# Hybrid RG-LRU and differential-attention block: k and q of heads 0 and 1 projected while the input arrives

## Chip, cores and metric

One core of a Trainium2 chip. The time is device microseconds of one launch; of several runs the median is given.

## What is computed

One decoder block on x, 2048 tokens of 1024 channels, float32. The reference, cut to its core:

```python
u = rmsnorm(h, pre_g[l])
z = einsum('bsd,df->bsf', u, w_in[l])                    # 1024 -> 8 x 1024
xr, zr, q, k, v, za, gm = split(z)                       # gm has 2 x 1024
y_r = rg_lru(causal_conv4(xr), ...) * silu(zr)           # gates from 64 x 64 blocks, scan over tokens
o   = diff_attention(q, k, v, lam)                       # 8 heads, causal: softmax(q0 k0) - lam softmax(q1 k1)
y_a = rmsnorm(o, subln_g[l]) * (1 - lam_init) * silu(za)
g_r, g_a = split(sigmoid(gm))
m = g_r * (y_r @ w_br_rnn) + g_a * (y_a @ w_br_attn)
h = h + rmsnorm(m @ w_out, post_g[l])
```

## The kernel before

Every large product is done in three fp16 products (high x high, high x low, low x high), so that 128 output channels by 512 tokens cost 3 x 8 = 24 matmuls of 512 columns (`mm3`, L187). Such a set is called a group here; done on 128 tokens at a time it is four pieces of 24 matmuls of 128 columns. Engines have short names: PE (matmul), DVE (vector), ACT (scalar), POOL (GpSimd), SP (its queue issues most transfers).

The work runs in four stages.

1. x phase. x comes in 16 tiles of 128 tokens, loaded five ahead. `x_stat` squares two tiles on ACT (L256) and turns the sums to scales on DVE, `x_fin` scales them on DVE (L266), makes the high half on ACT and the low half on DVE or POOL in turns (L270), and SP transposes both into `uT` (L276). Meanwhile PE works the first half row (8 tiles) of three blocks, x_r 0, z_r 0 and x_r 1, in pieces of 128 tokens (`in_half`, list `first`). Small constants, the LRU's gate weights (`gf`, `gw`) and the parameters (`rows`, `prm`) are loaded between the tiles.
2. LRU. Sixteen units, one for each block of 128 channels and half row: `xr_half` (48 matmuls of 512), convolution, `gates` (12 float32 matmuls), `zr_half` (48 matmuls), then the scan and the product. PSUM holds three tiles of 1024 (`lps`), each free once ACT and DVE have read it. Each unit also brings on one weight block: load (`wld`), norm on ACT (`wstat`, L156), scale by a one-column matmul (L162) and split into halves on ACT and DVE (`wfin`, L177, L178). The last loads are the first of the attention (`ahead`).
3. Attention. 128 units, one for each head and 128 queries: scores, exponentials, combination, transposes of the weights by DMA (`pt`), and the product with v two units later (`LAG`). Between them stand the remaining groups of the input projection, in a list `fills`: per head and chunk of 512 tokens k, q and two of v and za (`chunk_groups`), and the merge gates gm, 64 groups in all, of which 8 wait for the end. A running sum `acc` deals them out evenly over the units. A k or q group is split to fp16 halves (`split16`, L667, L668) and moved into K and Q by four or six transfers on SP. gm is written to DRAM.
4. Branch projections, merge and output projection from L1094 on.

The code is written in this order, but a scheduler orders the instructions of each engine; each engine then runs its own list strictly in that order and waits where an operand is missing.

Of the kernel before, what the change touches and what calls it, by code (L numbers as in the profile page):

```python
# [48 lines left out]
def kernel(  # L49
# [35 lines left out]
    gm_d = drp.tile([2 * KD, 128, S], F32, name="gm_d")  # L85

# [7 lines left out]
    with ExitStack():  # L94
# [65 lines left out]
        def w_scale(w, ps, fac, keep=None):  # L160
            """power of two that brings the block's norm close to 2^13 (a rough sum is enough for it)"""
            nc.tensor.matmul(ps[:, 0:1], ones16, w.ss, start=True, stop=True)  # L162
            tot = tl(1, "w_tot")
            nc.vector.tensor_scalar(out=tot, in0=ps[:, 0:1], scalar1=1e-30, scalar2=None, op0=ALU.max)
            w.sg, w.iv = keep or (tl(1, f"w_sg_{w.tag}"), tl(1, f"w_iv_{w.tag}"))
            pow2_bits(w.sg, tot, 13)
            pow2_inv(w.iv, w.sg)
            if keep is None:
                w.cz = wn_p.tile([128, 1], F32, tag=f"w_cz_{w.tag}", name="w_cz",
                                 bufs={"wg": 4, "agm": 3}.get(w.tag, 2))  # L170
                nc.vector.scalar_tensor_tensor(out=w.cz, in0=w.iv, scalar=fac, in1=cu, op0=ALU.mult, op1=ALU.mult)
# [15 lines left out]
        def mm3(ps, w, c0, n):  # L187
            """ps[f128, n] += w^T u over all of d, s in [c0, c0 + n)"""
# [7 lines left out]
        # ================= RG-LRU branch =================  # L196
        with ExitStack() as lx:
# [21 lines left out]
            def prep_g(gr):  # L219
                """power of two that keeps the scaled, normalised input in fp16's range"""  # L220
# [58 lines left out]
            # weight pipeline  # L279
            order = [(C_XR if i % 2 == 0 else C_ZR) + (i // 2) * 128 for i in range(2 * KD)]  # L280
            ahead = [("k", 0), ("q", 0), ("v", 0), ("za", 0)]
            order += [wkey_col(k) for k in ahead]
            ws = {}

            def wld(i):
                ws[i] = w_load(win, order[i], tag="wg" if i < 2 * KD else "a" + ahead[i - 2 * KD][0])
# [4 lines left out]
            def wfin(i):  # L291
                w_fin(ws[i], lpt.tile([128, 1], F32, tag="tot", name="tot"), 0.5 if i % 2 and i < 2 * KD else 1.0,
                      w16_at(i))

            first = []

            def in_half(b, hf, z, w):
                """PSUM tile of a half row of an x_r (z = 0) or z_r (z = 1) block"""
                if hf == 0 and 2 * b + z < 3:
                    if not first:  # L300
                        first.extend(lps.tile([128, HALF], F32, tag="ps", name="ps") for _ in range(3))
                        for i in range(HALF // 128):
                            for y_ in range(3):
                                mm3(first[y_][:, i * 128:(i + 1) * 128], ws[y_], i * 128, 128)
                    return first[2 * b + z]
# [3 lines left out]
                return ps  # L309

# [125 lines left out]
            with tc.issue_after(x_t[0]):  # L436
                wld(2)
            x_fin(2, 2, gb)
            x_stat(4, 2)
            wstat(2)  # L440
            wfin(2)
            x_fin(4, 2, gb)
            # per-channel vectors: rows of 128 channels, turned into columns
# [10 lines left out]
            x_stat(6, 2)  # L454
            x_fin(6, 2, gb)
            wld(3)
            x_stat(8, 2)
            x_fin(8, 2, gb)
            wstat(3)
            wfin(3)  # L460
# [8 lines left out]
            with tc.issue_after(x_last[1]):  # L469
                # block-diagonal gate weights, exact f32r hi/lo  # L470
# [8 lines left out]
            x_stat(10, 2)  # L479
            x_fin(10, 2, gb)  # L480
            x_stat(12, 2)
            x_fin(12, 2, gb)
            x_stat(14, 2)
            x_fin(14, 2, gb)
# [62 lines left out]
            seq = [(0, 0), (1, 0), (0, 1), (1, 1)] + [(b, hf) for b in range(2, KD) for hf in range(2)]  # L547
            when = {0: 2, 1: 2, 2: 3}
            for n, (b, hf) in enumerate(seq):
                xr_half(b, hf, ws[2 * b])  # L550
# [8 lines left out]
                if n > 0:  # L559
                    if n > 1:  # L560
                        wfin(n + 2)
                    wstat(n + 3)
                wld(n + 4)
                zr_half(b, hf, ws[2 * b + 1])
# [3 lines left out]
                if hf == 1:  # L568
                    ws.pop(2 * b)
                    ws.pop(2 * b + 1)  # L570
# [5 lines left out]
        # ================= differential attention and merge gates =================  # L576
# [3 lines left out]
        with ExitStack() as ax:  # L580
# [16 lines left out]
            wl = {k: ws[2 * KD + i] for i, k in enumerate(ahead)}  # L597
# [16 lines left out]
            def wadv(n):  # L614
                """weight blocks up to index n ready; two more on their way"""
# [16 lines left out]
            sc_h, nsc_h, kap_h = {}, {}, {}  # L632
# [20 lines left out]
            for k in ahead[:2]:  # L653
                after_w(k, wl[k])

# [42 lines left out]

            def g_va(h, c, g):
# [31 lines left out]
            def chunk_groups(h, c):  # L731
                return [("k", h, c), ("q", h, c), ("va", h, c, 0), ("va", h, c, 1)]
# [6 lines left out]
            def W_(nm, h):  # L739
                return [("w", nm, h)] if h < (2 * NH if nm == "gm" else NH) else []  # L740
# [30 lines left out]
            def fill():  # L771
# [5 lines left out]
                if g[0] == "w":  # L777
                    wadv(worder.index((g[1], g[2])))
# [195 lines left out]
        # ================= branch projections, merge, output projection =================  # L974
        with ExitStack() as bx_:
# [179 lines left out]
            # norm of the attention branch's rows, for a bound on the merged sum  # L1155
# [53 lines left out]
```

## Time and profile before

| what | value |
|---|---|
| median of 3 runs | 2503.14 us (2498.83 to 2506.12) |
| time of the first run | 2506.12 us |
| span of the profiled execution | 2506.1 us |
| PE busy | 2353.1 us, 94% |
| DVE, ACT, POOL busy | 62%, 49%, 27% |
| PE's granted clock, mean | 0.980 |
| DMA | 268.73 MB, mean 107 GB/s |

In the rows shown below, a window row gives a stretch in us, its length, then busy time and instructions of PE, PE's weight loads, DVE, ACT and POOL, the clock that PE was granted, the busy share of the DMA engines and GB/s. A timeline row gives start, length, engine, line, operation, out<-in, shapes, count, and in brackets the idle time before it with what ended it. A group row ends in count, then busy us, mean ns of one, idle time before. A transfer row ends in count, size of each and us from issue to landing.

### The profile page before, as it was taken

Reading aid. Unit: us, or ns where it says so; the run is one execution under the profiler, and the core shown is the slowest. Engines: PE = TensorE matmul, PEld = TensorE weight load, DVE = VectorE, ACT = ScalarE, POOL = GpSimd, SP = SyncE. Lnnn points to the kernel's source line nnn. Section 1 sums busy time; section 2 is a strip of 40 time slices with the busy share of each in tenths; the row PEclk is TensorE's granted clock in tenths of the full one; section 3 lists DMA queues with packets and bytes.
Section 4 is the critical chain, followed back from the end, with each engine's and each line's share of the span. In section 5 each row is a group of like instructions: output and inputs, shape, how many; then the busy total and the mean of one; then the engine's idle time right before and its main releaser. Section 6 shows DMA issues by size and latency. Waiting matters only on the chain. (4 is left out here: it accounts for less than half of the span.)

```text
span 2506.1 us, 41430 instructions
## 1 busy us (share of the span) xinstructions
PE 2353.1 (94%) x15240; PEld 1355.3 (54%) x15240; DVE 1548.4 (62%) x4316; ACT 1224.6 (49%) x2156; POOL 679.7 (27%) x415
## 2 busy tenths in 40 slices
PE   6789999999998999998998999999999899999998
PEld 5344444465665665665665655655655444444443
DVE  8877667668658566667567478468467244633323
ACT  5555545456547546556456457356456244312211
POOL 3443334212222212222222222223123133322211
PEclk9899999999999999999999999999999999999999
DMA  9511111235444534635535445445445854743202
GB/s 244 104 43 48 46 42 34 76 81 119 108 96 111 113 84 108 127 82 113 115 84 114 103 96 118 95 90 124 95 90 115 251 177 135 239 148 118 84 17 101
DMA packets 541323, 268.73 MB, mean 107 GB/s; under 512 B 370504, under 2 KB 518016, under 8 KB 541120
## 3 DMA queue, kind: packets, MB, share of 16 engines
q1 hardware_dynamic: 538144, 256.74, 42.6%
q0 software_dynamic: 2816, 9.08, 1.2%
q8 instruction: 119, 1.95, 0.3%
q14 instruction: 84, 0.69, 0.1%
q10 hardware_dynamic: 160, 0.27, 0.0%
HBM read 110.79 MB, written 41.94 MB: 61 GB/s over the span
## 5 line engine op out<-in xcount | busy, mean ns | idle before, releaser
L192 PEld LDWEIGHTS <-w 128*128 128x128 f16 x5040 | 475.9, 100 | 576.5 <-issue 89.2
L192 PE MATMUL mm<-uT,w 128*128 128x512 f16 x3072 | 705.1, 383 | 12.9 <-ACT gm L728 8.9
L877 POOL TENSOR_TENSOR e<-e,e 128x1024 f16<-128x1024 f32 (+2 forms) x192 | 317.0, 1666 | 970.6 <-ACT e L876 487.0
L851 ACT ACTIVATE e<-e,nb,sc_h 128x1024 f32<-128x1024 f32 (+7 forms) x384 | 376.1, 980 | 160.8 <-DVE nb L845 125.6
L826 DVE TENSOR_SCALAR_CACHE_REDUCE e<-sc 128x1024 f32<-128x1024 f32 (+7 forms) x352 | 305.2, 880 | 134.9 <-PE sc L814 122.3
L192 PE MATMUL ps<-uT,w 128*128 128x512 f16 (+1 forms) x1968 | 354.4, 345 | 26.1 <-ACT xr L318 17.7
L711 PE MATMUL mm<-wva,uT 128*128 128x256 f16 x3072 | 352.7, 275 | 3.3 <-DVE st L668 2.6
L1094 PE MATMUL psb<-yt,w 128*128 128x512 f16 x1536 | 332.9, 379 | 2.0 <-ACT w L177 1.5
L711 PEld LDWEIGHTS <-uT 128*128 128x128 f16 x3072 | 301.5, 99 | 48.8 <-issue 2.9
L814 PE MATMUL sc<-K,Q 128*128 128x512 f16 (+3 forms) x1280 | 287.2, 351 | 19.9 <-DVE e L826 13.8
L897 PE MATMUL o<-V,pt 128*128 128x128 f16 x3264 | 224.5, 222 | 38.4 <-DMA pt<-e 38.1
L1094 PEld LDWEIGHTS <-w 128*128 128x128 f16 x1536 | 149.1, 98 | 184.9 <-issue 3.9
L897 PEld LDWEIGHTS <-pt 128*128 128x128 f16 x3264 | 200.0, 99 | 72.8 <-DMA pt<-e 46.5
L876 ACT ACTIVATE e<-e 128x1024 f16<-128x1024 f32 (+2 forms) x192 | 150.1, 802 | 143.1 <-DVE e L874 118.5
L814 PEld LDWEIGHTS <-Q 128*128 128x128 f16 x1280 | 119.6, 99 | 133.2 <-issue 20.2
L874 DVE SCALAR_TENSOR_TENSOR e<-e,rs,e 128x1024 f32<-128x1024 f32 (+2 forms) x192 | 190.0, 1017 | 2.2
L1125 PE MATMUL psf<-wo,m 128*128 128x512 f16 x720 | 155.7, 379 | 0.0
L156 ACT ACTIVATE jk<-wst 128x1024 bf16<-128x1024 f32 x80 | 84.2, 1052 | 138.7 <-DMA wst<-in_w_in_dram 102.6
L1125 PEld LDWEIGHTS <-m 128*128 128x128 f16 x768 | 75.1, 98 | 90.6
L1098 DVE SCALAR_TENSOR_TENSOR t<-gt,psb 128x512 f32<-128x512 f32 x64 | 43.8, 686 | 120.2 <-PE psb L1094 100.1
L1148 ACT ACTIVATE jk<-psf 128x1024 bf16<-128x1024 f32 x15 | 15.4, 1024 | 134.0 <-PE psf L1125 69.4
L717 DVE SCALAR_TENSOR_TENSOR V<-mm,V 128x256 f16<-128x256 f32 x64 | 26.9, 421 | 85.7 <-ACT V L716 85.6
(247 smaller groups left out, 2417.3 us busy)
## 6 DMA issues: line engine op xcount, KB each, us to landing
wst<-in_w_in_dram SPq DMA_DIRECT2D x64, 512.0 KB, 4.5
xt<-in_x_dram SPq DMA_DIRECT2D x32, 512.0 KB, 4.5
gm_d<-gm SPq DMA_DIRECT2D x64, 256.0 KB, 2.7
gt<-gm_d SPq DMA_DIRECT2D x32, 512.0 KB, 3.8
K<-st SPq DMA_DIRECT2D x128, 64.0 KB, 2.0
Q<-st SPq DMA_DIRECT2D x64, 128.0 KB, 2.4
Q<-st SPq DMA_DIRECT2D x128, 64.0 KB, 2.1
ya_d<-yT SPq DMA_DIRECT2D x64, 128.0 KB, 2.0
```

The lines of the kernel that those rows point to most:

```text
L156: nc.scalar.activation(jk, w.st, AF.Square, accum_out=ss)
L192: nc.tensor.matmul(ps, w.t[:, a, k, :], uT[:, b, k, c0:c0 + n], start=(i == 0), stop=(i == 3 * KD - 1))
L711: nc.tensor.matmul(ps[:, j, :], uT[:, a, k, s0:s0 + 128], wt[:, b, k].rearrange("p t f -> p (t f)"), start=(i == 0), stop=(i == 3 * KD - 1))
L814: nc.tensor.matmul(ps[:, x * 128:x * 128 + m], Qt[h, t // 4][:, v, ci, q0:q0 + 128], K[:, ci, 0:m], start=(v == 0), stop=(v == 1))
L826: nc.vector.tensor_scalar(out=ev[:, 0:m], in0=ps[:, 0:m], scalar1=1.0, scalar2=None, op0=ALU.mult, op1=ALU.max, accum_out=u.mx[:, ci, col: ...
L851: nc.scalar.activation(ev[:, 0:nb * 128], ev[:, 0:nb * 128], AF.Exp, bias=nb_[:, ci:ci + 1], scale=sc_h[h], accum_out=u.sm[:, pi, ci:ci + 1])
L874: nc.vector.scalar_tensor_tensor(out=e0[:, 0:m], in0=e1v[:, 0:m], scalar=rs, in1=e0[:, 0:m], op0=ALU.mult, op1=ALU.add)
L876: nc.scalar.activation(e1[:, 0, 0:m], e0[:, 0:m], AF.Copy)
L877: nc.gpsimd.tensor_tensor(out=e1[:, 1, 0:m], in0=e0[:, 0:m], in1=e1[:, 0, 0:m], op=ALU.subtract)
L897: nc.tensor.matmul(o, pt[:, a, kb % 8, :], V[:, kb % 4, b, :], start=(kb == 0 and i == 0), stop=(kb == n - 1 and i == 2))
L1094: nc.tensor.matmul(ps, w.t[:, p, k, :], y_t[b][:, q, k, sl], start=(i == 0), stop=(i == 3 * KD - 1))
L1125: nc.tensor.matmul(pn[n], m16[:, a, j, ms], wo[:, b, j, ns], start=(j == 0 and a == 0 and b == 0), stop=(j == KD - 1 and a == 1))
```

## The change

k and q of heads 0 and 1 (four blocks, `early`) become the first weight blocks. `piece(n, i)` works block n on tile i as soon as the tile is there, for all 16 tiles; after each four tiles the halves are split (ACT, DVE) and written to a DRAM tensor `kq_d` by a transfer on ACT's queue. The list `first` goes: all 16 LRU blocks now run in the LRU stage in whole half rows, in plain order. In the attention heads 0 and 1 have no k and q groups: `load_kq` brings K and Q from DRAM by six transfers a chunk. The blocks loaded ahead are now gm 0, gm 1, v 0 and za 0; three gm groups come before the first unit, and the rest of gm is dealt out so that each head has about the same number of groups in all. The small constants stand behind the last x tile.

```diff
+EARLY = 2
+    kq_d = drp.tile([2, EARLY, 2, 128, S], F16, name="kq_d")
...
-            ahead = [("k", 0), ("q", 0), ("v", 0), ("za", 0)]
+            early = [(nm, h) for h in range(EARLY) for nm in ("k", "q")]
+            order = [wkey_col(k) for k in early]
+            order += [(C_XR if i % 2 == 0 else C_ZR) + (i // 2) * 128 for i in range(2 * KD)]
+            ahead = [("gm", 0), ("gm", 1), ("v", 0), ("za", 0)]
...
-                if hf == 0 and 2 * b + z < 3:
-                    if not first:
-                        first.extend(lps.tile([128, HALF], F32, tag="ps", name="ps") for _ in range(3))
-                        for i in range(HALF // 128):
-                            for y_ in range(3):
-                                mm3(first[y_][:, i * 128:(i + 1) * 128], ws[y_], i * 128, 128)
-                    return first[2 * b + z]
...
+            def piece(n, i):
+                if i % 4 == 0 and n % 2 == 0:
+                    eps_[n // 2] = lps.tile([128, 2, CH], F32, tag="ps", name="ps")
+                ps = eps_[n // 2][:, n % 2]
+                mm3(ps[:, (i % 4) * 128:(i % 4 + 1) * 128], ws[n], i * 128, 128)
+                if i % 4 == 3:
+                    c = i // 4
+                    st = le.tile([128, 2, CH], F16, tag="xr", name="kst")
+                    nc.scalar.activation(st[:, 0], ps, AF.Copy, scale=p2(-14))
+                    nc.vector.scalar_tensor_tensor(out=st[:, 1], in0=ps, scalar=p2(-14), in1=st[:, 0],
+                                                   op0=ALU.mult, op1=ALU.subtract)
+                    nc.scalar.dma_start(out=kq_d[n % 2, n // 2, :, :, c * CH:(c + 1) * CH].rearrange("l p s -> p l s"),
+                                        in_=st)
...
+            for i in range(2, 16):
+                for n in range(NE):
+                    piece(n, i)
+                if i % 2 == 0 and i + 4 < 16:
+                    x_stat(i + 4, 2)
+                    x_fin(i + 4, 2, gb)
...
+            wfin(4)
+            wfin(5)
...
-            seq = [(0, 0), (1, 0), (0, 1), (1, 1)] + [(b, hf) for b in range(2, KD) for hf in range(2)]
+            seq = [(b, hf) for b in range(KD) for hf in range(2)]
...
+            def load_kq(h, c):
+                s0 = c * CH
+                t = kp.tile([128, 2, CH], F16, tag="K", name="K")
+                for l in range(2):
+                    nc.sync.dma_start(out=t[64 * l:64 * l + 64], in_=kq_d[0, h, l, :, s0:s0 + CH].rearrange(
+                        "(i p) s -> p i s", i=2))
...
-                return [("k", h, c), ("q", h, c), ("va", h, c, 0), ("va", h, c, 1)]
+                return ([("l", h, c)] if h < EARLY else [("k", h, c), ("q", h, c)]) + [("va", h, c, 0), ("va", h, c, 1)]
...
-            fills = W_("k", 0) + W_("q", 0) + c0[0:1] + W_("v", 0) + c0[1:2] + W_("za", 0) + c1[0:2] + c0[2:4]
-            fills += W_("gm", 0) + W_("gm", 1) + c1[2:4]
-            done = 0
+            fills = W_("gm", 0) + W_("gm", 1) + c0[0:1] + gms[0:1] + W_("v", 0) + gms[1:2] + W_("za", 0) + gms[2:3]
+            fills += c0[1:] + c1
+            done = 3
...
-                upto = len(gms) * (h + 1) // NH
+                own = 8 * min(h + 1, EARLY) + 16 * max(0, h + 1 - EARLY)
+                upto = len(gms) if h == NH - 1 else min(len(gms), 3 + tot * (h + 1) // NH - own)
```

Two places in the engines' lists. Names are those of the code with a buffer's number; lines of the changed kernel are one or two higher before the LRU stage and up to 46 higher behind.

DVE, the end of the x phase, before: the scaling of x tiles 12 and 13 (L266), then work of the first LRU blocks (halo, g, xc) around the low half of tile 12 (L270) and the next tiles' statistics (L257).

```order
L266 SCALAR_TENSOR_TENSOR xt_381<-xt_381,rx_499,gb_111 128x1024
L266 SCALAR_TENSOR_TENSOR xt_414<-xt_414,rx_499,gb_111 128x1024
L322 COPY halo_1196<-xr_1193 128x3
L387 SCALAR_TENSOR_TENSOR g_1209<-g_1209,ps_615 128x1024
L327 SCALAR_TENSOR_TENSOR xc_1198<-xr_1193,prm_448,xc_1198 128x1024
L270 TENSOR_TENSOR u16_521<-xt_381,u16_521 128x1024
L322 COPY halo_1215<-xr_1212 128x3
L327 SCALAR_TENSOR_TENSOR xc_1198<-xr_1193,prm_448,xc_1198 128x1024
L327 SCALAR_TENSOR_TENSOR xc_1217<-xr_1212,prm_448,xc_1217 128x1024
L257 TENSOR_SCALAR vx_533<-ssx_532 128x2
```

The same place after, at the last two tiles: the splits `kst` (L320) of the early blocks stand between and behind the scaling (L268) and the low half (L272). ps_805 holds k and q of head 0, tokens 512 to 1023; the PSUM tile that PE calls ps_1332 reuses its place.

```order
L320 SCALAR_TENSOR_TENSOR kst_1195<-ps_805,kst_1195 128x512
L268 SCALAR_TENSOR_TENSOR xt_938<-xt_938,rx_1614,gb_113 128x1024
L268 SCALAR_TENSOR_TENSOR xt_1161<-xt_1161,rx_1614,gb_113 128x1024
L272 TENSOR_TENSOR u16_1636<-xt_938,u16_1636 128x1024
L528 MEMSET sp4_2242 128x8
L117 TENSOR_SCALAR ciu_3045<-cu_106 128x1
L320 SCALAR_TENSOR_TENSOR kst_1223<-ps_805,kst_1223 128x512
```

The LRU work has left this place, and evictions that PE waits for stand behind the input's own steps.

SP, the start of the attention, before: K and Q of chunk 0 are moved from the splits, then chunk 1.

```order
L680 DMA K_3898<-st_3895 64x512 x2
L681 DMA K_3898<-st_3895 64x512 x2
L680 DMA K_4007<-st_4004 64x512
L693 DMA Q_3952<-st_3949 64x2x512
L694 DMA Q_3952<-st_3949 64x512
L695 DMA Q_3952<-st_3949 64x512
```

After: K of six chunks comes first, with three writes of gm between, and Q of chunk 0 behind them.

```order
L730 DMA K_5137<-kq_d_60 64x2x512 x2
L730 DMA K_5440<-kq_d_60 64x2x512
L769 DMA gm_d_59<-gm_5170 128x512
L730 DMA K_5440<-kq_d_60 64x2x512
L730 DMA K_5673<-kq_d_60 64x2x512 x2
L730 DMA K_6130<-kq_d_60 64x2x512 x2
L730 DMA K_6782<-kq_d_60 64x2x512 x2
L769 DMA gm_d_59<-gm_5222 128x512
L730 DMA K_7709<-kq_d_60 64x2x512 x2
L769 DMA gm_d_59<-gm_5272 128x512
L735 DMA Q_5140<-kq_d_60 64x2x512 x4
```

The first Q, which the first scores read, now stands behind the write of the third gm group instead of behind its own split.

More of the change, by code (lines that the diff above doesn't have):

```diff
@@ L277, in x_fin @@
                                                              in_=u16[:, hl_]).ins
-            order = [(C_XR if i % 2 == 0 else C_ZR) + (i // 2) * 128 for i in range(2 * KD)]
-            ahead = [("k", 0), ("q", 0), ("v", 0), ("za", 0)]
+            early = [(nm, h) for h in range(EARLY) for nm in ("k", "q")]
+            order = [wkey_col(k) for k in early]
+            order += [(C_XR if i % 2 == 0 else C_ZR) + (i // 2) * 128 for i in range(2 * KD)]
+            ahead = [("gm", 0), ("gm", 1), ("v", 0), ("za", 0)]
             order += [wkey_col(k) for k in ahead]
+            NE = len(early)
             ws = {}
             def wld(i):
-                ws[i] = w_load(win, order[i], tag="wg" if i < 2 * KD else "a" + ahead[i - 2 * KD][0])
+                ws[i] = w_load(win, order[i], tag="wk" if i < NE else "wg" if i < NE + 2 * KD else "a" + ahead[i - NE - 2 * KD][0])
             def wstat(i):
@@ L309, in in_half @@
                 return ps
+            esc = cst.tile([128, EARLY, 2], F32, name="esc")
+            eps_ = {}
+            def piece(n, i):
[11 more added lines that the diff above has]
+                                        in_=st)
             xc_t = {}
@@ L437 @@
                 wld(2)
+                wld(3)
             x_fin(2, 2, gb)
+            for i in range(2):
+                for n in range(2):
+                    piece(n, i)
             x_stat(4, 2)
-            wstat(2)
-            wfin(2)
-            x_fin(4, 2, gb)
+            for n in range(2, 4):
+                wstat(n)
+                wfin(n)
+                for i in range(2):
+                    piece(n, i)
+            for h in range(EARLY):
+                nc.vector.scalar_tensor_tensor(out=esc[:, h, 0:1], in0=ws[2 * h + 1].cz, scalar=0.125 * p2(28),
+                                               in1=ws[2 * h].cz, op0=ALU.mult, op1=ALU.mult)
+                nc.vector.tensor_scalar(out=esc[:, h, 0:1], in0=esc[:, h, 0:1], scalar1=1e-34, scalar2=None, op0=ALU.max)
+                nc.vector.tensor_scalar(out=esc[:, h, 1:2], in0=esc[:, h, 0:1], scalar1=-1.0, scalar2=None, op0=ALU.mult)
+            x_fin(4, 2, gb)
+            for i in range(2, 16):
+                for n in range(NE):
+                    piece(n, i)
+                if i % 2 == 0 and i + 4 < 16:
+                    x_stat(i + 4, 2)
+                    x_fin(i + 4, 2, gb)
+                if i == 9:
+                    wld(4)
+                    wld(5)
+                if i == 12:
+                    wstat(4)
+                    wstat(5)
+            wfin(4)
+            wfin(5)
+            wld(6)
+            wstat(6)
+            wld(7)
             rows = le.tile([65, 128], F32, tag="rows", bufs=1, name="rows")
@@ L594 @@
             ps_m = ax.enter_context(tc.tile_pool(name="ps_m", bufs=2, space=PSUM))
-            wl = {k: ws[2 * KD + i] for i, k in enumerate(ahead)}
+            wl = {k: ws[NE + 2 * KD + i] for i, k in enumerate(ahead)}
             wva_t = {}
@@ L630, in wadv @@
                         wpos[0] += 1
-            sc_h, nsc_h, kap_h = {}, {}, {}
+            sc_h = {h: esc[:, h, 0:1] for h in range(EARLY)}
+            nsc_h = {h: esc[:, h, 1:2] for h in range(EARLY)}
+            kap_h = {}
             def after_w(key, w):
@@ L651, in after_w @@
                                             op0=ALU.mult, op1=ALU.mult)
-            for k in ahead[:2]:
-                after_w(k, wl[k])
             Kt, Qt, Vt, Gt = {}, {}, {}, {}
@@ L697, in g_q @@
                 Qt[h, c] = t
+            def load_kq(h, c):
[4 more added lines that the diff above has]
+                        "(i p) s -> p i s", i=2))
+                Kt[h, c] = t
+                t = qp.tile([128, 2, 2, CH], F16, tag="Q", name="Q")
+                for a, l, v in ((0, 0, 0), (0, 1, 1), (1, 1, 0), (1, 0, 1)):
+                    nc.sync.dma_start(out=t[64 * a:64 * a + 64, v], in_=kq_d[1, h, l, :, s0:s0 + CH].rearrange(
+                        "(i p) s -> p i s", i=2))
+                Qt[h, c] = t
             def g_va(h, c, g):
@@ L739, in W_ @@
             def W_(nm, h):
[L740 removed]
+                return [("w", nm, h)] if h < (2 * NH if nm == "gm" else NH) and (nm, h) not in early else []
             c0, c1 = chunk_groups(0, 0), chunk_groups(0, 1)
[L743 to L745 removed]
+            fills = W_("gm", 0) + W_("gm", 1) + c0[0:1] + gms[0:1] + W_("v", 0) + gms[1:2] + W_("za", 0) + gms[2:3]
+            fills += c0[1:] + c1
+            done = 3
+            tot = 8 * EARLY + 16 * (NH - EARLY) + len(gms) - done
             for h in range(NH):
[L747 removed]
+                own = 8 * min(h + 1, EARLY) + 16 * max(0, h + 1 - EARLY)
+                upto = len(gms) if h == NH - 1 else min(len(gms), 3 + tot * (h + 1) // NH - own)
                 seg = gms[done:upto]
```

43 lines of the change are left out of this document (15 added, 28 removed).

## Prediction

> **What bounds the kernel now.** I read the page's engine rows and slices first, then the stretches, then TensorE's (PE's) own waits by place.
>
> ```profile
> span 2506.1 us, 41430 instructions
> ...
> PE 2353.1 (94%) x15240; PEld 1355.3 (54%) x15240; DVE 1548.4 (62%) x4316; ACT 1224.6 (49%) x2156; POOL 679.7 (27%) x415
> ...
> PE   6789999999998999998998999999999899999998
> ```
> ```profile
> 0.00:115.00 115.00, 71.78 (x709) 54.74 (x710) 95.27 (x249) 59.25 (x83) 41.69 (x37) 0.91 0.85 185
> 115.00:480.00 365.00, 345.14 (x1542) 167.20 (x1541) 262.83 (x307) 197.61 (x186) 136.66 (x74) 0.97 0.13 42
> 560.00:2100.00 1540.00, 1462.67 (x10612) 902.78 (x10610) 976.09 (x3196) 843.56 (x1692) 385.39 (x238) 0.99 0.51 114
> ```
> PE carries the end nearly everywhere (first busy column; the clock is the third number from the right). Only the first 115 us are half empty, 71.8 of 115. So moving work helps only as far as it fills that stretch without opening holes elsewhere. All sums are against this execution: its span, 2506.1, stands 3.0 above the median of the three runs, 2503.14.
>
> What holds PE early, in its timeline (start, length, waits in brackets):
>
> ```profile
> 34.85 12.73 PE L192 MATMUL ps<-uT,w 128*128 128x128 f16 x196 [2.22 <-DMA uT<-u]
> ...
> 52.63 12.06 PE L192 MATMUL ps<-uT,w 128*128 128x128 f16 x213
> 71.12 18.30 PE L192 MATMUL ps<-uT,w 128*128 128x512 f16 x72 [6.43 <-ACT xr L318]
> ...
> 97.35 0.77 PE L351 MATMUL ps<-xh,gwh 128*128 128x512 f32 x1 [7.91 <-DVE gwh L513]
> ...
> 114.15 22.46 PE L192 MATMUL ps<-uT,w 128*128 128x512 f16 x96 [4.39 <-ACT xr L318]
> ...
> 141.93 20.88 PE L192 MATMUL ps<-uT,w 128*128 128x512 f16 x96 [0.65 <-ACT xr L318]
> ```
> A 128-wide matmul costs 12.06/213 = 56.6 ns in a full stream, a 512-wide one 20.88/96 = 217.5 ns. So a group of 24 x 512 is 5.22 us, and done in four pieces it is 5.43. After the 6.43 us wait the 512-wide ones ran at 254 ns: such a hole costs 2.6 us more behind it (72 x 37 ns).
>
> **x phase, part by part.** Before, PE works three blocks on eight tiles (576 small matmuls). Now it works four on sixteen: 1,536. Up to 34.85 the streams are alike (97 small ones now). Then come 196 at the 12.73 us of that row, to 47.6. The other 1,243 at 56.6 ns are 70.4 us: 118.0, if nothing waits. Does x arrive in time, and are the PSUM tiles free?
>
> ```profile
> 33.50 1.28 DVE L178 SCALAR_TENSOR_TENSOR w<-wst,w_sg_wg,w 128x1024 f16<-128x1024 f32 x1
> ...
> 49.48 2.48 DVE L266 SCALAR_TENSOR_TENSOR xt<-xt,rx,gb 128x1024 f32<-128x1024 f32 x2
> ...
> 60.26 2.48 DVE L266 SCALAR_TENSOR_TENSOR xt<-xt,rx,gb 128x1024 f32<-128x1024 f32 x2
> ...
> 69.81 2.48 DVE L266 SCALAR_TENSOR_TENSOR xt<-xt,rx,gb 128x1024 f32<-128x1024 f32 x2
> ...
> 87.89 2.48 DVE L266 SCALAR_TENSOR_TENSOR xt<-xt,rx,gb 128x1024 f32<-128x1024 f32 x2
> ```
> ```profile
> 76.03 1.06 ACT L256 ACTIVATE jk<-xt 128x1024 bf16<-128x1024 f32 x1 [1.06 <-DMA xt<-in_x_dram]
> ```
> ```profile
> 40.00:60.00 20.00, 18.94 (x338) 18.82 (x336) 16.83 (x41) 10.69 (x15) 8.30 (x10) 1.00 1.14 229
> ```
> A pair of x tiles is scaled every 9 to 11 us; the DMA engines are full (share 1.14). The last pair was held to 87.9 by the LRU work between it and its statistics, which is now gone. Its square ran at 76.0, so its scaling can come near 80. At 5.4 us a tile PE is slower than x, so x does not hold it. PSUM does: three tiles serve, and the two splits that free a tile stand in DVE's queue behind the scaling of later x (front rows: kst_1223 behind both L268 and u16_1636).
> - The tile ps_854 needs kst_745, behind tile 10 (60.26 + 1.2 + 0.7 = 62, or 61 since DVE has less in between); PE is there at 47.6 + 197 x 0.0566 = 58.8: 2 us.
> - ps_1332 needs kst_1223. PE is there 337 matmuls later, at 80. The split is ready at 82 if the last x loads earlier than before, at 88 if it loads at 76 as before; I take 85: 5 us, plus 1 for the clock.
> - 684 more small ones take 38.7: 124.7. Then the first LRU block's weights are split only after the last tiles (a scale, 1.1 on ACT, 1.3 on DVE): 2.5 us. First LRU matmul: 127 (120.5 with no PSUM wait, 136 if the last x comes 9 us later).
>
> - The constants now start after the last x tile: 14 small loads on POOL's queue, and DVE's casts of the LRU's gate weights wait for them ahead of kst_1699, which frees the tile of ps_1808.
>
> ```profile
> 57.65 1.85 POOL L474 MEMSET gf<- 128x1024 f32 x2
> 59.44 0.75 POOL L476 DMA_DIRECT2D gf<-in_lru_wa_dram  x1
> ```
> ```profile
> gf<-in_lru_wx_dram POOLq DMA_DIRECT2D x2, 128.0 KB, 5.7
> ```
> POOL's last x at 88, 14 issues at up to 0.75 and two clears of 0.9, 5.7 to land, 2 us of casts: 108. PE is there at 86 + 375 x 0.0566 = 107: 0 to 4, I take 0. Six tiny scale operations on DVE (esc) hide behind x's loads; without that cover they are under 1 us.
>
> The 16 splits themselves move from the attention, 0.59 on ACT and 0.69 on DVE each:
>
> ```profile
> L668 DVE SCALAR_TENSOR_TENSOR st<-mm,st 128x512 f16<-128x512 f32 x58 | 39.7, 685 | 54.1 <-ACT st L667 54.1
> ```
> ```profile
> L667 ACT ACTIVATE st<-mm 128x512 f16<-128x512 f32 x58 | 34.0, 586 | 54.2 <-PE mm L192 53.3 <-DMA K<-st 0.8
> ```
> The 16 writes to DRAM go out on ACT's queue, each waiting there for DVE's half; behind them stand the squares of later x, which wait for x's load at those times anyway. Nearest row below; four of the 16 go before the last x is in, at 1.1 us each by the 229 GB/s above: some 4 us at the end of x, inside the 82 to 88.
>
> ```profile
> gm_d<-gm SPq DMA_DIRECT2D x64, 256.0 KB, 2.7
> ...
> K<-st SPq DMA_DIRECT2D x128, 64.0 KB, 2.0
> ```
> In the attention 80 small transfers become 48 loads on SP's queue: nothing gained or lost, since the loads have a whole chunk of lead; if that fails, a Q wait of 1 to 2 us a chunk, 8 chunks.
>
> **LRU.** It has all 32 half blocks now, not 29.
>
> ```profile
> 219.69 0.18 PE L162 MATMUL tot<-w_s,ones 128*128 128x1 bf16 x1
> ...
> 424.31 2.98 PE L192 MATMUL mm<-uT,w 128*128 128x512 f16 x13
> ...
> 447.65 0.58 PE L351 MATMUL ps<-xh,gwh 128*128 128x512 f32 x1
> ...
> 465.99 0.39 PE L353 MATMUL ps<-xh,gwl 128*128 128x512 f32 x1
> 469.55 6.71 PE L192 MATMUL mm<-uT,w 128*128 128x512 f16 x24 [3.16 <-DVE w_tot L164]
> ...
> 487.67 0.28 PE L711 MATMUL mm<-wva,uT 128*128 128x256 f16 x1 [0.60 <-ACT wva L177]
> ```
> ```profile
> 136.26 0.58 PE L351 MATMUL ps<-xh,gwh 128*128 128x512 f32 x1
> ```
> Eight units lie between the first two rows: 25.6 us each. Twelve lie between 136.26 and 447.65: 25.95, start included. I take 25.75. Now: three half blocks (31.3) and 24 late small ones (1.4) bring the first gates to 159.8; 14 units, 360.5, the last but one to 520.3; the rest 18.6 as before (447.65 to 466.2): 538.9 against 466.2, **+72.7** (units alone +/-3).
>
> **Handover.** v and za weights wait for memory that the last LRU block still holds:
>
> ```profile
> 485.43 1.15 ACT L177 ACTIVATE wva<-wst,w_sg_av 128x1024 f16<-128x1024 f32 x1 [2.90 <-DVE y L396]
> ```
> That release comes the same time behind the last gates. Between them PE had 72 matmuls of k and q; the new list puts 48 of the gate projections (gm) there. One group's time is empty: **+5.2** (0 to 7, with Q's load, queued last on SP, at the high end).
>
> **Attention.** 16 groups of 5.22 us leave PE: **-83.5**. But these groups also fill the time in which a unit's chain runs:
>
> ```profile
> PE o L897 <- DMA pt<-e: 37.2, 28, 3.2
> PE sc L814 <- DVE e L826: 13.8, 9, 4.4
> ```
> (560 to 1970 us: total, times, longest.) The waits cluster at the borders of heads, where long units end and short ones give little cover. 176 groups instead of 192 is 8% less cover, 0.6 us of some 7.5 a unit, 1.25 for the two units between a score and its product. All 37 waits longer by that: +46. None: 0 (splits leaving DVE and ACT could even save a few). I take one longer wait a head, **+10**, nearest the windows, where every head already loses about the same.
>
> Sum: 72.7 + 5.2 - 83.5 + 10 = **+4.4 us**, the x phase's 127 being in the first term. On the median that is 2507, less than the 0.3% (7.5 us, the spread of the three runs) that a measurement here can tell from no change.
>
> A rule against the change: in the Trainium skill, TensorE: Matmul & The Clock Gate, section Back-to-back issue gap, a stream of weight load and matmul pairs sustains about 81 ns at 128 columns. By it the 1,536 would take 124 us, some 37 more, and the sum would come near 2540: an estimate from that page. The 213 in 12.06 us are such a stream and disagree.
>
> **Rivals.**
> - *Faster, 0.31.* Evictions come in time (xr at 120.5, -6.5) and the gates dealt anew keep the borders covered (0 for 10): -12, 2491. For: x's scaling loses the LRU work in front of it; DVE and ACT are 62% and 49% busy. Against: in-order DVE.
> - *Slower by the attention, 0.20.* The pt chain takes over at the borders: waits grow by 30 rather than 10: 2527. It decides from about +14 there. For: 37 us of such waits already; against: the scheduler re-deals PE's order.
> - *Slower by the x phase, 0.12.* kst_1223 comes after 93 us because the writes crowd full DMA engines: xr at 136, +9: 2516.
> - *Slower by the small matmuls, 0.02.* PE does not keep 56.6 ns over 1,500 small ones but stays at the 12.73/196 = 65 ns of the first row: 1,243 x 8.4 ns, +10: 2517. Against: the row of 213.
>
> **The numbers.** No measurable change 0.35, faster 0.31, slower 0.34 (0.20 + 0.12 + 0.02). The likeliest is 2507. The range runs from a little below the faster rival, 2484 (units at 25.6 too), to just above the attention's, 2532.
>
> **What would show it.** Right: small matmuls dense from 35 to 125 with short waits on DVE's kst near 60 and 82; first LRU matmul near 127; last gates near 539; a hole of some 5 us more before the first va; idle time per head up by about 1. Wrong: a first LRU matmul outside 120 to 136, units off 25.6 to 26, or pt waits outside 35 to 70.

## The result, and the profile after

The changed kernel takes 2572.3 us (median of 4 runs, 2568.4 to 2575.0), the kernel before 2502.8 beside it (4 runs, 2498.8 to 2506.1). The ratio is 1.0277, with a 95% interval of 1.0264 to 1.0291: slower by 70 us, and far outside the predicted 2484 to 2532. The profiled runs span 2566.6 and 2506.1 us, so the traces have 60.5 us to explain (the profiled run was the shortest of its four for the changed kernel and the longest of its four for the kernel before).

The front went as predicted, or better. TensorE (PE) in the x phase of the changed kernel, then at the end of the LRU and the start of the attention, from the timeline (start, length, instruction, count, idle time before it):

```profile
37.46 24.56 PE L194 MATMUL ps<-uT,w 128*128 128x128 f16 x392 [3.76 <-DMA uT<-u]
62.37 14.23 PE L194 MATMUL ps<-uT,w 128*128 128x128 f16 x252 [0.35 <-DVE kst L320]
80.66 43.20 PE L194 MATMUL ps<-uT,w 128*128 128x128 f16 x745 [4.05 <-DVE kst L320]
...
127.17 11.44 PE L194 MATMUL ps<-uT,w 128*128 128x512 f16 x70 [0.88 <-DVE w L180]
```
```profile
510.87 0.59 PE L365 MATMUL ps<-xh,gwh 128*128 128x512 f32 x1
...
529.21 0.39 PE L367 MATMUL ps<-xh,gwl 128*128 128x512 f32 x1
532.74 5.34 PE L194 MATMUL mm<-uT,w 128*128 128x512 f16 x24 [3.14 <-DVE w_tot L166]
...
549.58 0.61 PE L751 MATMUL mm<-wva,uT 128*128 128x256 f16 x2 [5.38 <-ACT wva L179]
```
The waits for kst are 0.35 and 4.05 us, near 62 and 81. The LRU's last gates end at 529.6 instead of 466.2, and the first v group starts 61.9 us later than before (549.58 against 487.67).

The attention then should have given some 80 us back. It gave almost nothing: from the last gates to the steady stream of the branch stage (a row of 20 branch matmuls begins at 2027.19 before, at 2087.07 after) it took 1561.0 us before and 1557.5 after. Behind that the two traces are equal (478.9 and 479.5 to the end). PE's waits in the attention of the changed kernel (560 to 2040 us: total, times, longest):

```profile
PE o L943 <- DMA pt<-e: 53.8, 45, 4.5
PE tot L164 <- DVE w_s L160: 32.0, 8, 10.0
PE sc L860 <- DVE e L872: 22.9, 14, 3.2
PE sc L860 <- DVE mx L876: 6.2, 5, 1.9
```
Against the rows of before in the prediction, the wait for the transposed probabilities (pt) grew by 16.6 us and that for the exponentials' tiles (e) by 9.1. No row names the K and Q that now come back from DRAM (`kq_d`), so that detour did not hold PE here. The second row is new in this size: **32.0 us in 8 waits, up to 10.0 long, for `w_s`**. Before, it was this (560 to 1970 us):

```profile
PE tot L162 <- DVE w_s L158: 4.3, 2, 2.3
```
The one that waits is the one-column matmul `tot`, which sums a weight block's norm. Windows of 180 us show where; here the kernel before, then the changed one (length, busy time and count of each engine, granted clock, DMA share, GB/s):

```profile
1100.00:1280.00 180.00, 169.90 (x1279) 107.23 (x1278) 119.66 (x405) 101.96 (x210) 41.73 (x27) 0.99 0.51 104
```
```profile
560.00:740.00 180.00, 171.01 (x1342) 113.92 (x1339) 131.26 (x446) 109.90 (x231) 45.40 (x32) 0.98 0.51 110
...
920.00:1100.00 180.00, 158.31 (x1118) 97.70 (x1117) 110.94 (x323) 90.81 (x169) 42.66 (x23) 0.97 0.44 94
1100.00:1280.00 180.00, 157.14 (x1208) 100.31 (x1206) 120.94 (x396) 99.28 (x204) 45.99 (x28) 0.93 0.49 101
1280.00:1460.00 180.00, 160.34 (x1233) 104.23 (x1232) 114.05 (x389) 95.64 (x202) 41.14 (x26) 0.95 0.43 89
```
Heads 0 and 1, which lost their k and q groups, got shorter: from the first product with v of a head to the next head's, 154 and 163 us instead of 168 and 180. Heads 2, 3 and 4 took 223, 197 and 192 instead of 182, 180 and 180. Of head 2's 41 us more, some 21 are four groups that now run in it (27 for 23); heads 3 and 4 run no more groups than before (22 and 21 for 22 and 22). In these windows PE loses 11 to 14 us of busy time each against the kernel before (172.5, 169.9 and 171.1), and the granted clock falls to 0.93.

One of the long waits, engine by engine, in the changed kernel's timeline:

```profile
1213.48 0.51 SPq L147 DMA_DIRECT2D wst<-in_w_in_dram  x1
...
1238.50 1.89 PE L860 MATMUL sc<-K,Q 128*128 128x512 f16 x8
...
1239.76 1.24 ACT L897 ACTIVATE e<-e,nb,sc_h 128x1024 f32<-128x1024 f32 x1 [3.32 <-DVE nb L891]
...
1245.23 5.08 DVE L920 SCALAR_TENSOR_TENSOR e<-e,rs,e 128x1024 f32<-128x1024 f32 x2
...
1247.27 1.04 ACT L158 ACTIVATE jk<-wst 128x1024 bf16<-128x1024 f32 x1
...
1250.23 0.14 DVE L160 CAST w_s<-w_ss 128x1 bf16<-128x1 f32 x1
...
1250.43 0.16 PE L164 MATMUL tot<-w_s,ones 128*128 128x1 bf16 x1 [10.03 <-DVE w_s L160]
1250.45 6.68 PE L194 MATMUL mm<-uT,w 128*128 128x512 f16 x21
```
The block is v of head 4. Its load went out at 1213.5 and had landed at 1218.1 (the next load, at 1232.2, is the next block's). Its norm on ACT (L158) stands in ACT's queue behind the exponentials of three units and runs only at 1247.3, 29 us after the landing; the cast of the result on DVE stands behind 5.08 us of L920. All that time `tot`, next in PE's queue, holds the 21 projection matmuls behind it, whose weights had been split by 1227.6 at the latest: 10 us of empty PE. The Trainium skill says why they can't pass (TensorE: Matmul & The Clock Gate, section Step-by-step: what each phase is for): matmuls stay in program order, only weight loads are pulled ahead. The trace agrees: not one of them starts before 1250.45.

The other wait of this length, at 1444.5, is of the same kind: landed at 1411.9, norm at 1441.3. Three of the shorter ones (5.1, 2.9 and 1.5 us) are not: there the norm ran within 2.1 us of the landing, and the block had only just arrived. So 20 of the 32 us are owed to the place of a norm in ACT's and DVE's queues, and not to a late load.

What the change did to the order: the list of entries (groups, and the weight blocks before them) deals out 12 and 13 gate groups in heads 0 and 1 and 4 or 5 in the later ones, where it was 7 in each. A unit takes from the list at a mean pace, and takes more when it needs a chunk's groups. Counted from the list, in heads 2 to 6 nearly all groups are now such forced ones: 6, 4, 4 and 6 at the starts of the four chunks of heads 3 to 5 (10 once, in head 2) and hardly one at the other units, where before the forced ones were 5 to 14 of 22 to 24 a head. In these bursts the blocks for k, q, v and za stand one group (5 us) apart, and v or za at times directly behind a gate block. That spacing is not new: in the list before, 30 of 47 blocks stand at most one group behind the block before them, now 27 of 43. New is that the groups stand in bursts and not beside the units. How this brings a norm so late into ACT's queue the list does not show, and no run took it apart. The scheduler spreads a burst a little, but most of the largest is there in one piece, 42 us and eight groups without one score matmul:

```profile
906.15 20.88 PE L194 MATMUL mm<-uT,w 128*128 128x512 f16 x96
926.87 0.17 PE L164 MATMUL tot<-w_s,ones 128*128 128x1 bf16 x1
927.32 10.52 PE L194 MATMUL mm<-uT,w 128*128 128x512 f16 x48 [0.28 <-DVE w_tot L166]
937.67 10.64 PE L751 MATMUL mm<-wva,uT 128*128 128x256 f16 x96
948.15 1.25 PE L860 MATMUL sc<-K,Q 128*128 128x512 f16 x8
```

### The profile page after: what moved, and what is told of

Its sections match the earlier page's. It is cut to its first block, busy times and chain, and to the rows that moved or that the text cites. A ratio compares the mean times of both kernels' runs of the same rounds, so it can differ in the third digit from the quotient of the medians.

```text
span 2566.6 us, 42775 instructions
## 1 busy us (share of the span) xinstructions
PE 2368.3 (92%) x15960; PEld 1391.3 (54%) x15960; DVE 1547.9 (60%) x4316; ACT 1226.7 (48%) x2156; POOL 674.7 (26%) x415
## 5 line engine op out<-in xcount | busy, mean ns | idle before, releaser
L194 PEld LDWEIGHTS <-w 128*128 128x128 f16 x5760 | 505.8, 100 | 542.5 <-issue 81.3
L194 PE MATMUL mm<-uT,w 128*128 128x512 f16 x2688 | 622.5, 384 | 8.7 <-ACT gm L768 5.0
L194 PE MATMUL ps<-uT,w 128*128 128x128 f16 (+1 forms) x3072 | 434.0, 306 | 20.1 <-DMA uT<-u 7.4
L897 ACT ACTIVATE e<-e,nb,sc_h 128x1024 f32<-128x1024 f32 (+7 forms) x288 | 282.0, 980 | 118.6 <-DVE nb L891 84.8
L860 PE MATMUL sc<-K,Q 128*128 128x512 f16 (+3 forms) x1280 | 292.9, 358 | 32.4 <-DVE e L872 22.9
L943 PE MATMUL o<-V,pt 128*128 128x128 f16 x3264 | 235.9, 225 | 54.0 <-DMA pt<-e 53.8
L943 PEld LDWEIGHTS <-pt 128*128 128x128 f16 x3264 | 206.5, 101 | 109.0 <-DMA pt<-e 79.3
L1140 PEld LDWEIGHTS <-w 128*128 128x128 f16 x1536 | 149.7, 98 | 188.3 <-issue 7.2
L922 ACT ACTIVATE e<-e 128x1024 f16<-128x1024 f32 (+2 forms) x192 | 149.2, 801 | 147.4 <-DVE e L920 125.7
L920 DVE SCALAR_TENSOR_TENSOR e<-e,rs,e 128x1024 f32<-128x1024 f32 (+2 forms) x192 | 196.2, 1049 | 1.9
L158 ACT ACTIVATE jk<-wst 128x1024 bf16<-128x1024 f32 x80 | 84.3, 1054 | 141.0 <-DMA wst<-in_w_in_dram 105.3
L897 ACT ACTIVATE e<-e,nb,esc 128x1024 f32<-128x1024 f32 (+7 forms) x96 | 94.0, 981 | 39.5 <-DVE nb L891 30.8
L970 POOL TENSOR_TENSOR y<-y,y 128x512 f16<-128x512 f32 x32 | 40.0, 1251 | 218.9 <-ACT y L967 166.1
```

The source lines that it names most:

```text
L158: nc.scalar.activation(jk, w.st, AF.Square, accum_out=ss)
L194: nc.tensor.matmul(ps, w.t[:, a, k, :], uT[:, b, k, c0:c0 + n], start=(i == 0), stop=(i == 3 * KD - 1))
L860: nc.tensor.matmul(ps[:, x * 128:x * 128 + m], Qt[h, t // 4][:, v, ci, q0:q0 + 128], K[:, ci, 0:m], start=(v == 0), stop=(v == 1))
L897: nc.scalar.activation(ev[:, 0:nb * 128], ev[:, 0:nb * 128], AF.Exp, bias=nb_[:, ci:ci + 1], scale=sc_h[h], accum_out=u.sm[:, pi, ci:ci + 1])
L920: nc.vector.scalar_tensor_tensor(out=e0[:, 0:m], in0=e1v[:, 0:m], scalar=rs, in1=e0[:, 0:m], op0=ALU.mult, op1=ALU.add)
L922: nc.scalar.activation(e1[:, 0, 0:m], e0[:, 0:m], AF.Copy)
```

## The experiments

Four readings of this were open. C: the cover that left with 16 groups is what costs. D: the bursts cost, because units elsewhere have no groups beside them. W: the waits at the blocks' norms cost. F: the new front costs more than the trace of one run shows. All ratios below are to the kernel before, run beside each kernel on the same chip, with 95% intervals.

**1. The dealing alone, on the kernel before.**
```diff
-                upto = len(gms) * (h + 1) // NH
+                upto = done + [12, 13, 4, 5, 5, 4, 5, 8][h]
```


> The kernel before, with one number per head changed: the groups of gate projections stand as 12, 13, 4, 5, 5, 4, 5, 8 a head in the list instead of 7 each. Same work, same x phase, no k or q in DRAM. Theory D (the new dealing holds the attention up: in heads 2 to 6 nearly all projection groups run in bursts, 4 to 12 at the start of a chunk, because the next unit needs them, and none beside the other units): the list then gives bursts of 7, 12, 6 and 7 groups as the changed kernel has them, so most of the 72 us by which its heads 2 to 6 ran over comes back here: 2553 to 2583 us. Theory C (what costs is only the cover that k and q took along): the number of groups in the attention is unchanged, so 2495 to 2511. Theory W (only the weight blocks that stand closer together cost, the 32 us of waits for a block's norm): 2523 to 2538.

Measured: 2584.7 us, ratio 1.0314 [1.0299, 1.0329]: 81 us slower, slower even than the changed kernel, and just above D's range. Its list is still more bunched than the changed kernel's (counted from the list, 26 forced groups and a burst of 12 in head 2, for 21 and 10), so it shows what such a dealing can cost, not the changed kernel's share to the microsecond. C is out as the main cause: no group has left this kernel. W by its waits alone (20 to 35 us) falls short. Its waits, 640 to 2040 us:

```profile
PE o L897 <- DMA pt<-e: 57.7, 40, 8.6
PE sc L814 <- DVE e L826: 27.8, 14, 5.2
PE tot L162 <- DVE w_s L158: 24.1, 7, 10.0
```

**2. The changed kernel's list, at each head's own pace.** `bnd` holds where each head's stretch of the list ends.
```diff
-            acc = ACC0
+            acc = bnd[0] - PACE
...
-                acc += per * (u.t + 1 + FB) / wsum
+                acc += (bnd[u.h + 1] - bnd[u.h]) * (u.t + 1 + FB) / wsum
```


> The changed kernel with the same list, word for word; only the pace at which the units take from it is each head's own length of list instead of one mean (26.5 entries a head). Counted from the list, the groups that run ahead of a unit because it needs them fall from 21, 20, 20, 20 in heads 2 to 5 to 8, 9, 9, 13, and the largest burst from 10 to 4. Theory D: 35 to 60 us come back, 2512 to 2537. Theory C: as the changed kernel, 2565 to 2575. Theory W (blocks still as close together in the list): 2555 to 2572.

Measured: 2554.4 us, 1.0200 [1.0185, 1.0216]. Only 18 us come back, just below W's range and far from D's: half of the forced groups of heads 2 to 5 are gone (39 left of 81), but the waits for norms are not (640 to 2040 us):

```profile
PE o L947 <- DMA pt<-e: 61.4, 34, 10.0
PE tot L164 <- DVE w_s L160: 23.2, 7, 10.3
```

**3. No wait for the norm of a new block.** Same list, same pace, same bursts; the scale is a power of two, for which a rough sum is enough.
```diff
-            nc.tensor.matmul(ps[:, 0:1], ones16, w.ss, start=True, stop=True)
+            nc.tensor.matmul(ps[:, 0:1], ones16, w.ss if ss is None else ss, start=True, stop=True)
...
+                              ss=wl[worder[wpos[2] - 1]].ss)
```


> The changed kernel; in the attention the scale of a weight block is taken from the norm of the block before it, so that TensorE no longer waits there for the norm of a block that has only just arrived (the 8 waits, 32 us together, longest 10.0). Theory W: 25 to 35 us come back, 2537 to 2547. Theory D: the burst ends earlier but the units behind it have no groups beside them all the same and the next wait comes sooner; 0 to 15 back, 2557 to 2572. Theory C says nothing of it: 2540 to 2572.

Measured: 2513.9 us, 1.0036 [1.0023, 1.0049]. 58 us come back, more than any theory gave, and nearly twice the 32 us of the waits themselves. One long wait is left (11.2 us). The rows of 640 to 2040 us show what went with the waits:

```profile
PE o L944 <- DMA pt<-e: 37.4, 37, 3.1
PE sc L861 <- DVE e L873: 17.4, 14, 3.6
PE tot L164 <- DVE w_s L160: 12.3, 2, 11.2
```
In the same window the changed kernel has 50.4, 22.9 and 32.0. So 20 us fewer at the norms bring 18.5 fewer at pt and e. What the held PE delays is not only groups: the scores of the next unit stand in the same queue, start late, and then their exponentials and transposes are late too. Counted from the traces, from the last gates to the first branch matmul, all waits over 0.15 us fell from 137.9 to 94.6 us, and what the matmuls lost while the granted clock stood at half fell from 36.1 to 23.6 (last section): 43 and 12 us, which is the whole gain between the two traces there (55.5). The burst of 240 projection matmuls is still there (900 to 942 us), so that burst by itself is cheap.

**4. Even dealing, own pace, norms as they were.** Edit 2 with `PACE` 6 in place of 8 (the list starts two entries further ahead), and:
```diff
-                upto = len(gms) if h == NH - 1 else min(len(gms), 3 + tot * (h + 1) // NH - own)
+                upto = done + [12, 8, 5, 5, 4, 5, 5, 9][h]
```


> The changed kernel with the gate groups dealt as 12, 8, 5, 5, 4, 5, 5, 9 a head, so that every head's stretch of the list (its own chunks 2 and 3, and chunks 0 and 1 of the next head) holds about 20 groups, and with the pace of each head's own list. Groups forced ahead of a unit: 1, 1, 2, 4, 5, 3, 4 a head, largest burst 2. Theory D: the attention gives back its 83 us less a few, so 2503 + 62 (the later start) - 75 = 2490, 2480 to 2503. Theory C: 2560 to 2575, since the same 16 groups are missing. Theory W: 2540 to 2560.

Measured: 2500.9 us, 0.9993 [0.9982, 1.0004]: 71 us come back without touching a single wait. This is inside D's range and below W's, but it doesn't part the two, for the waits went as well: the norms are ready in time (1.5 us in 1 wait), with blocks that stand no further apart in groups (28 of 43 at most one group behind the block before):

```profile
PE o L947 <- DMA pt<-e: 44.3, 35, 4.4
PE mm L194 <- ACT gm L768: 11.3, 3, 7.0
...
PE tot L164 <- DVE w_s L160: 1.5, 1, 1.5
```

**5. The dealing on the kernel before, without the wait for norms.** Edits 1 and 3.

> The kernel before with the groups of gate projections dealt 12, 13, 4, 5, 5, 4, 5, 8 a head (2584.7 us alone) and, in the attention, a block's scale taken from the norm of the block before it. Theory W2 (the dealing costs because weight blocks then come due in bursts, TensorE is held at a block's norm, and what its holding delays comes on top): most of the 81 us come back here too, 2505 to 2530. Theory D2 (most of the loss is the units without groups beside them; the two repairs on the changed kernel add up by chance): 20 to 35 come back, 2550 to 2565.

Measured: 2522.0 us, 1.0076 [1.0056, 1.0096]. 63 of the 81 us come back in a kernel that has neither the new front nor the missing groups: W2. Longest wait 10.0 before, now:

```profile
PE o L898 <- DMA pt<-e: 36.8, 33, 4.5
PE sc L815 <- DVE e L827: 19.2, 13, 4.3
PE tot L162 <- DVE w_s L158: 6.1, 4, 3.0
```

**6. Even dealing with the old pace.** The edit of 4 without that of 2.

> The changed kernel with the even dealing alone (12, 8, 5, 5, 4, 5, 5, 9 a head), the old pace and the wait for the norm as they were. Forced groups a head by count: 1, 4, 12, 14, 12, 9, 7, 7, largest burst 5; gate groups stand again between the chunks of heads 1 and 2 and fewer ahead of head 2. Theory W2: the holding goes where the blocks get further apart, which it does only in head 1 and 2; 2515 to 2545. Theory D2 (forced groups count): about 60 of 100 forced groups remain against 116, 2530 to 2550.

Measured: 2518.1 us, 1.0056 [1.0035, 1.0077]: 54 us back, at the lower end of W2's range. The pace, worth 18 us alone, adds 17 to this (with `PACE` 6). For the dealing the order of the list matters more than how it is paced:

```profile
PE tot L164 <- DVE w_s L160: 7.3, 6, 3.1
```

**7. Edits 2, 3 and 4 together.**

> The changed kernel with the even dealing, the pace of each head's own list, and the scale from the norm of the block before. Both theories: the waits for a norm are 1.5 us already without the last part, so it is worth 0 to 5: 2494 to 2503. Theory W2 would see more than 5 only if a held TensorE were still hidden under other names.

Measured: 2485.0 us, 0.9935 [0.9919, 0.9952], the best of all: 17 us under the kernel before. The repair of the norms brought 16 us where 0 to 5 were expected, although the waits named `w_s` were only 1.5 us. Counted from the traces (560 to 2030 us), gaps of over 1 us between the starts of two matmuls sum to 89.0 us in kernel 4 and 70.5 here; waits for pt and e are 44.3 and 11.1 there, 39.0 and 7.0 here (640 to 2040 us). Part of the holding at norms did go on under another name in kernel 4: all waits of `tot` there are 7.2 us, 1.5 put down to `w_s`, 2.4 to gm and 3.4 to `pb`; in that last one the cast of the block's norm ran only 0.2 us before `tot`. Here they are 2.4, all for gm. So some 5 us were held at norms, and pt and e bring 9 more.

```profile
PE o L948 <- DMA pt<-e: 39.0, 35, 4.2
PE mm L194 <- ACT gm L769: 11.8, 4, 7.0
PE sc L865 <- DVE e L877: 7.0, 8, 2.5
```

**8. The new front alone.** The x phase and LRU of the changed kernel; the attention as before, with all k and q computed.
```diff
-            return ([("l", h, c)] if h < EARLY else [("k", h, c), ("q", h, c)]) + ...
+            return [("k", h, c), ("q", h, c)] + ...
...
-                upto = len(gms) if h == NH - 1 else min(len(gms), 3 + tot * (h + 1) // NH - own)
+                upto = len(gms) * (h + 1) // NH
```


> The x phase and the LRU as in the changed kernel (k and q of heads 0 and 1 worked as x arrives and written to DRAM), the attention as in the kernel before: k and q of all heads are computed in it, 7 gate groups a head, nothing is read back. So the new front stands alone. By the trace of the changed kernel the first v group starts 61.9 us later and nothing behind it changes: 2503 + 62 = 2565, 2560 to 2570. By the prediction's terms (72.7 at the last gates, 5.2 at the handover) it would be 2581.

Measured: 2562.4 us, 1.0243 [1.0221, 1.0264]: 60 us. The front costs what the trace showed, no more: F is out. The changed kernel saves itself 16 groups of 5.22 us and is still 10 us slower than this one.

**9. The kernel before, without the wait for norms.** Edit 3 alone.

> The kernel before with one part changed: in the attention a block's scale is taken from the norm of the block before it. It says what the early k and q are worth by themselves, with the holding at norms out of both. Theory W2: TensorE waits there only 4.4 us for a norm (2 times), with little behind it: 0 to 8 back, 2494 to 2503; the changed kernel with even dealing, pace and the same repair took 2485.0, so the early k and q would be worth 9 to 18 us. Rival (the repair helps any dealing, and the change is worth nothing): 2480 to 2490.

Measured: 2490.6 us, 0.9949 [0.9935, 0.9964]. 12 us come back where 0 to 8 were expected, 0.6 us above the rival's range, by which the repair helps any dealing and the change is worth nothing: the old dealing had some of this too. Head 5 of the kernel before, at 191 us its longest, takes 175 here. In 480 to 2060 us its waits for pt were 38.1 and for w_s 6.8; now:

```profile
PE o L898 <- DMA pt<-e: 33.0, 28, 3.0
PE tot L162 <- DVE w_s L158: 1.8, 1, 1.8
```
With the same repair in both, the change (with even dealing and pace) is worth 2490.6 - 2485.0 = 5.6 us by the medians, some 3.5 by the ratios, whose intervals overlap: not told from nothing.

**10. A third tile for gate groups**, paid for with one of two tanh tiles, on kernel 7.
```diff
-                t = sp.tile([128, CH], F32, tag="gm", name="gm")
+                t = sp.tile([128, CH], F32, tag="gm", bufs=3, name="gm")
...
-                th = sp.tile([128, 2, 128], F32, tag="th", name="th")
+                th = sp.tile([128, 2, 128], F32, tag="th", bufs=1, name="th")
```


> The best version so far (2485.0) with three buffers instead of two for a gate group's output tile and one instead of two for the tanh of a v group (the memory it needs). TensorE's waits for ACT's gm there are 14 us (11.8 and 2.4), 7.0 of them one wait behind the last head, where a tile waits for its write to DRAM. If these lie on the path: 5 to 12 back, 2473 to 2480. If the write to DRAM only passes the wait on: 2482 to 2488. If the single tanh tile holds the v groups: above 2488.

Measured: 2487.7 us, 0.9942 [0.9925, 0.9958]: no gain. In 480 to 2060 us the wait for gm fell from 12.6 to 8.0, and that for pt rose from 39.2 to 45.7, which fits the case in which the wait is passed on; the single tanh tile was not tried apart from it.

```profile
PE o L948 <- DMA pt<-e: 45.7, 38, 5.2
PE mm L194 <- ACT gm L769: 8.0, 3, 5.0
```

Put side by side (us, medians; "-": not run):

| | norm of its own block | norm of the block before |
|---|---|---|
| before, 7 gate groups a head | 2502.4 | 2490.6 |
| before, dealt 12, 13, 4, 5, ... | 2584.7 | 2522.0 |
| changed kernel | 2572.3 | 2513.9 |
| changed, own pace | 2554.4 | - |
| changed, even dealing | 2518.1 | - |
| changed, even dealing and pace | 2500.9 | 2485.0 |

On the kernel before, the new dealing costs 81 us where PE waits for norms and 31 where it doesn't: about 50 of the 81 come through the norms. The other 31 stay when the norms are repaired; that they are the bursts (D) is what is left over, and was not tried by itself.

## Why the prediction was wrong

- **The x phase: right.** The first LRU matmul was predicted at 127, waits of 2 and 5 us on the splits near 60 and 82; the rows show 127.17 behind a first pair at 125.7, and 0.35 and 4.05 us. 745 small matmuls took 43.20 us, 58 ns each: the 56.6 ns held, and the rival of 65 ns did not. Nor did the rule of the Trainium skill that the prediction weighed (TensorE: Matmul & The Clock Gate, section Back-to-back issue gap: 81 ns). That the sum hit 127 is in part luck: the waits were 2.6 us shorter than the 7 taken, and a slower start (392 matmuls at 62.7 ns, behind a wait of 3.76 us for uT) made up for it. The second wait also stood elsewhere. PE met it 84 matmuls ahead of ps_1332 by the prediction's count, and a split that ran at 79.91, ahead of the last scaling of x (80.52), let it go; at ps_1332 itself, at 86.8, PE did not wait, for the splits behind the scaling were done by 85.9.
- **The LRU: right in kind, 9 us too dear.** First gates predicted at 159.8, in the trace at 159.0. The 14 units then took 351.9 us (to 510.87), 25.1 each instead of 25.75: +63.4 for +72.7. That is outside 25.6 to 26, one of the prediction's own signs of being wrong. The kernel before had waits and a lower clock in its first units (0.95 granted in 160 to 260 us, now 0.98), and these most likely went into the mean.
- **The handover: the hole was right (5.38 us), the term was not.** The v weights come 18 us behind the last gates where it was 19, so the first v group came 20.0 us behind the gates and not 21.5: -1.5 instead of +5.2. Putting other work than k and q in front of a wait of fixed end costs nothing there; what is missing in front of it only appears as a hole.
- **The attention: the step that failed.** "16 groups leave PE, -83.5" and "one longer wait a head, +10" were to leave -68.3 together with the handover; the trace has -3.5, so 64.8 us were missed. The removal itself held: heads 0 and 1 became 14 and 18 us shorter. The +10 for waits is what failed. Counted from the traces, from the last gates to the first branch matmul, PE's waits of over 0.15 us went from 77.8 to 137.9 us, and what its matmuls lost at half clock from 22.9 to 36.1: 60 and 13 us more. The sum lacked a term for the re-dealt gate groups, and one for `tot`, which they leave waiting for norms. It gave them none, and the faster rival even counted the dealing as a gain at the borders. Kernel 1 shows that such a dealing alone costs 81 us, kernels 3 and 5 that 58 and 63 us come back once `tot` no longer waits. With the dealing evened and paced and the norms out of the way, a remainder c is left: 60 for the front, less 83.5, plus c makes the -5.6 between kernels 9 and 7, so c is about 18, against the +10 taken and a bound of +46. It need not be lost cover: in that stretch of the two traces the waits differ by 2 us only (69.4 and 71.7), the loss at half clock by 8. What brings it was not tried.
- **The rival "slower by the attention"** had the right place and sign, with waits +30; its mechanism (the pt chain takes over because cover is missing) is not the one found. pt waits were 53.8, inside the 35 to 70 given, and so that test of the prediction could not see what happened: the new wait was at a matmul of one column, which the list of what would show it wrong did not name.
- **What could have been seen.** The order in which the changed kernel issues its work was at hand. Heads 2 to 6 with their groups in bursts stand in it; the row of 219.69 in the prediction shows such a `tot` in PE's queue, and the kernel before already waited 4.3 us there.

## What to carry to other kernels

Small matmuls that stand in PE's queue to serve another engine (a norm, a scale) are gates for everything behind them: price each by when its input can be ready on the engines that make it, not by its 0.16 us. Look not only at when the data land but at where the steps between (here the norm on ACT and the cast on DVE) stand in their engines' queues, or take a value that is already there; the runs tried only the second. When groups of filler work are dealt anew, list per unit what runs and how much is forced, since the same amount in bursts cost up to 81 us here. And repair such a wait in both kernels before crediting a change: 12 of the 17 us by which the best version beats the kernel before came from the wait and would have come without the change.

## What the runs showed of the hardware

- **A hole costs more than its length, through the clock.** The changed kernel around the wait shown above, in stretches cut where the granted clock changed (the clock is the number after POOL's count):

```profile
1227.20:1230.60 3.40, 1.22 (x6) 0.48 (x7) 3.23 (x8) 1.40 (x7) 3.40 (x2) 1.00 0.66 125
1230.65:1237.40 6.75, 5.02 (x28) 3.25 (x28) 4.71 (x17) 5.15 (x9) 0.25 (x1) 0.50 0.62 146
1237.45:1244.20 6.75, 2.94 (x26) 1.77 (x25) 5.13 (x19) 4.44 (x7) 0.00 (x0) 1.00 0.09 32
1244.30:1254.45 10.15, 4.02 (x11) 1.46 (x11) 9.48 (x22) 8.07 (x14) 8.85 (x5) 0.50 0.63 123
```
  PE ended its last matmul before the wait at 1240.4; the clock fell 3.9 us later. The first matmul behind the wait came at 1250.43, those of 512 columns then started 427 ns apart, and 4.1 us later the clock rose and they started 216 apart. The Trainium skill (TensorE: Matmul & The Clock Gate, section Part 1: The HAM clock gate) has half clock after at least one idle window of about 3.4 us, until at least one as long a busy one: the trace agrees at this wait in both lengths. What I had not expected is the first row: the clock fell behind it too, though PE was busy in it for 1.2 of 3.4 us, and its longest gap was 1.9 us. This is the rule here rather than the exception: in 13 of the 17 falls between 560 and 2040 us PE had been busy for 0.3 to 1.4 us of the 3.4 before. Several short waits in a row counted here like one long one. From the last gates to the first branch matmul the clock stood at half for 105.8 us in the changed kernel, 54.6 before and 64.9 in kernel 3; matmuls that started in that time lost 36.1, 22.9 and 23.6 us against the usual distance of their form.
- **DVE ran 2 to 3 times slower in some cases beside POOL.** L920 of the changed kernel takes 1.15 us at 896 columns and 1.28 at 1024 with POOL idle (78 cases), and 3.0 to 3.2 in the 4 cases, two of each size, in which POOL worked all the time. POOL's being busy is not all of it: in 13 more cases of 1024 columns POOL worked for half to four fifths of the time, and ten of them still took 1.28, three 2.1. Two slow ones held the cast above; their rows there (1245 to 1251 us: busy, mean ns):

```profile
L920 DVE SCALAR_TENSOR_TENSOR e<-e,rs,e 128x896 f32<-128x896 f32 x1 | 3.0, 3005 | 0.0
L920 DVE SCALAR_TENSOR_TENSOR e<-e,rs,e 128x1024 f32<-128x1024 f32 x1 | 2.1, 2148 | 0.0
```
  This was read from the trace alone; no run tried it, and what parts the slow cases from the others is open.
